# Two groups of gate columns staged in the stick-breaking and general buffers of one mixer and expert kernel

## Chip, cores and metric

The kernel runs on one core of a Trainium2 chip. The metric is the device time of one execution in microseconds (us). The kernel before took 3502.78 us, the median of three runs (3499.89 to 3507.8).

## What is computed

A decoder layer over 1024 tokens of width 1024: a norm, a token mixer with three branches (stick-breaking attention, sparse attention, a gated recurrence), a merge and an output projection, then a PEER feed-forward layer, then a final norm. The part that matters here is the last:

```python
def peer_ffn(x, w_q, sub_keys, u_tab, v_tab):
    ...
        best_s, pos = lax.top_k(cand, K)
        eidx = jnp.take_along_axis(cand_idx, pos, axis=-1)
        gate = jax.nn.softmax(best_s, axis=-1)
        ug = u_tab[eidx]
        vg = v_tab[eidx]
        hpre = jnp.einsum("nd,nhkd->nhk", xc, ug).astype(f32)
        act = (gate * jax.nn.gelu(hpre, approximate=False)).astype(x.dtype)
        return jnp.einsum("nhk,nhkd->nd", act, vg)
```

Each token has 8 heads with 16 chosen experts each, out of 16384, and each chosen expert has a gate.

## The kernel before

The 1024 tokens are cut into four parts of 256 (`PARTS`). The mixer runs part by part, as one long list of small steps (`items`), between which projections, merges and routing steps (`pieces`) are placed by estimated loads of TensorE (PE) and VectorE (DVE). The order on each engine is then settled at build time by a scheduler; on the chip each engine works through its own queue strictly in that order.

The feed-forward layer is done in two ways. For the tokens of parts 0 and 3 (256 + 256), the rows of the chosen experts are gathered one slot at a time from DRAM by GpSimd (POOL) and multiplied and summed on VectorE (`gather_tile`, lines 1149 to 1161; `gacc` is the running sum, `v_33` the row of slot 33). The gathers are spread over the whole later kernel. For the 512 tokens of parts 1 and 2 (`DENSE`), all 16384 experts are computed in 128 blocks of 128 on TensorE: `gemm1` multiplies a block of u with the tokens (`g`, line 265), ACT applies gelu (`ge`, line 1400), VectorE multiplies with the gates (`gt`, line 1434), the result is split into two half-precision parts (`ac`, lines 220 and 221), and a second product with v adds into PSUM (`acc`, line 1441). Raw weights come as `uraw` and `vraw` by SyncE's (SP's) queue and are split into two parts by ACT and VectorE (`us`, `vs`).

This needs the gates as a dense table, token by expert. `spread_pieces` (lines 1207 to 1230) makes it, four tokens a step: VectorE builds `hot` tiles of zeros and ones in one of four general buffers (tag w4, which `uraw` uses too), TensorE multiplies them into a PSUM tile `gb` (pool `ps_mm`, two buffers), ACT copies that with one instruction into a staging tile (line 1226). After four steps, 16 tokens are complete, and ACT's queue issues the write of 1 MB to the table `d_G` in DRAM (line 1228). There are 32 groups of 16 tokens. Three staging tiles serve them: two in `stages`, which share the space of the table of normalized tokens `h2` that the expert loop loads, and a third, `stage`, with one buffer. Groups 0 to 29 take turns over the three; groups 30 and 31 use the third only, since `stages` has by then to be released for `h2`. So groups 29, 30 and 31 all use `stage`:

```python
u = n0 // 16 % 3 if n0 < TH - 32 else 2
stage[0] = per.tile([128, 128, 16], F32, tag="stage", name=f"stage{n0}") if u == 2 else stages[:, u]
```

Behind the last group stands the beginning of the expert loop: three blocks of `gemm1`, then for each block k: `gemm1` of block k + 3, the load of `vraw`, at the first of every eight blocks two loads of gates (`gt_0` for the first 256 dense tokens, `gt_16` for the others, 1 MB each), the gate product, and the acc matmuls. The output projection of part 3 (`pj_wo`, `tr_wo`) is placed between blocks.

The stick-breaking branch keeps its keys in two buffers (`sbk`, 4 KB a partition each) and its values in one (`sbv`, 4 KB), and the whole mixer shares eight general buffers of 2 KB (tag `at`). After the last stick-breaking head the first three are not used again. They belong to pool `w2`, which is released together with `stage` before the expert loop's own buffers (`late`) are opened.

Of the kernel before, what the change touches and what calls it, by code (L numbers as in the profile page):

```python
# [10 lines left out]
F32 = mybir.dt.float32  # L11
# [5 lines left out]
AF = mybir.ActivationFunctionType  # L17
# [18 lines left out]
TH = 512  # L36
# [8 lines left out]
SGT, SA = 2.0 ** 10, 2.0 ** 4  # L45
# [26 lines left out]
def trunk(ctx: ExitStack, tc: tile.TileContext, a: dict, out: bass.AP):  # L72
    nc = tc.nc
    V, S, G, P = nc.vector, nc.scalar, nc.gpsimd, nc.tensor
# [13 lines left out]
    per = mix.enter_context(tc.tile_pool(name="per", bufs=1))  # L88
# [14 lines left out]
    def W4(name, shape=(128, 1024), dt=F32):  # L103
        return w4.tile(list(shape), dt, tag="w4", name=name)

    def W2(name, shape=(128, 512), dt=F32, tag="at", bufs=AT):
        return (wk if tag in ("at", "pre", "sg") else w2).tile(list(shape), dt, tag=tag, name=name, bufs=bufs)
# [98 lines left out]
    def dram(name, shape, dt=F32):  # L206
        return drm.tile(list(shape), dt, name=name)
# [92 lines left out]
    stages = hpl.tile([128, 2, 128, 16], F32, tag="h2", name="stages", bufs=1)  # L300
# [429 lines left out]
    def hg_pieces(h, pt, st):  # L730

        nm = f"hg{h}_{pt.i}"
        n = pt.n

        def pi():
            ps = proj(B_HI + h, hTs[pt.i], f"i_{nm}", pt)
            st["iT"] = PRE(f"iT_{nm}", pt)
            S.activation(st["iT"], ps, AF.Copy, scale=PS)

        def pi2():  # L740
            tr = transposed(st["iT"], f"i_{nm}", True)
            st["iv"] = W2(f"iv_{nm}", (128, n), tag="iv", bufs=2)
            S.activation(st["iv"], tr, AF.Copy)

        def pg(i, blk):
            if i == 0:
                st["raw"] = W2(f"raw_{nm}", (128, 3, n), tag="raw", bufs=2)
            ps = proj(blk + h, hTs[pt.i], f"r{i}_{nm}", pt)
            S.activation(st["raw"][:, i], ps, AF.Copy, scale=PS)

        return [pi, pi2, lambda: pg(0, B_HF), lambda: pg(1, B_HQ), lambda: pg(2, B_HG)]
# [126 lines left out]
    def gate_pieces(r, pt, st):  # L878

        def one(i):  # L880
            if i == 0:
                st["mg"] = W2(f"mg{r}_{pt.i}", (128, 6, pt.n), tag="mg", bufs=1)
            j, br = divmod(r * 6 + i, 3)
            ps = proj(B_MG + br * 8 + j, hTs[pt.i], f"mg{br}_{j}_{pt.i}", pt)
            S.activation(st["mg"][:, i], ps, AF.Copy, scale=PS)  # L885

        return [lambda i=i: one(i) for i in range(6)]
# [315 lines left out]
    d_G = dram("d_G", (32, 128, 128, 16))  # L1203
# [4 lines left out]
    def spread_pieces(pt):  # L1208

        stage = {}  # L1210

        def four(q):
            n0 = pt.t0 - TD + q * 4
            if q % 4 == 0:
                u = n0 // 16 % 3 if n0 < TH - 32 else 2
                stage[0] = per.tile([128, 128, 16], F32, tag="stage", name=f"stage{n0}") if u == 2 else stages[:, u]
            sp = spread[pt.i][:, :, q * 4:q * 4 + 4]
            hs = W4(f"hot{n0}", (128, 4, 128, 4), F16)
            V.tensor_tensor(hs[:, 0:2], iorep.unsqueeze(1).to_broadcast([128, 2, 128, 4]), sp[:, 0:2].unsqueeze(2).to_broadcast([128, 2, 128, 4]), op=ALU.is_equal)
            V.tensor_tensor(hs[:, 2:4], hs[:, 1:2].to_broadcast([128, 2, 128, 4]), sp[:, 2:4].unsqueeze(2).to_broadcast([128, 2, 128, 4]), op=ALU.mult)  # L1220
            ps = ps_mm.tile([128, 4, 128], F32, tag="mm", name=f"gb{n0}")
            for n in range(4):
                P.matmul(ps[:, n, :], hs[:, 0, :, n], hs[:, 2, :, n], start=True, stop=False)  # L1223
                P.matmul(ps[:, n, :], hs[:, 0, :, n], hs[:, 3, :, n], start=False, stop=True)
            m0 = q % 4 * 4
            S.activation(stage[0][:, :, m0:m0 + 4], ps.rearrange("p n i -> p i n"), AF.Copy, scale=SA / SGT)  # L1226
            if q % 4 == 3:
                nc.scalar.dma_start(d_G[n0 // 16], stage[0])

        return [lambda q=q: four(q) for q in range(pt.n // 4)]  # L1230

# [23 lines left out]
    def chain(fns, after=-100, before=1 << 30, deps=(), vector=False, to=None):  # L1255

        res = []
        for fn in fns:
            p = Piece(fn, after, before, list(deps) + res[-1:], vector)
            res.append(p)  # L1260
        (pieces if to is None else to).extend(res)
        return res

    def at(pt, r, kind, table, other=-10):
        i = pt.i * 4 + r
        return table.get((i // 4, i % 4, kind), other)
# [3 lines left out]
    for pt in PARTS:  # L1270
        i = pt.i
# [4 lines left out]
        for r in range(4):  # L1276
# [9 lines left out]
            p = chain(hg_pieces(r, pt, hg), ripe(at(pt, r - 2, "hg", end)), start[i, r, "hg"], here)  # L1286
            mg = None
            if r:
                mg = ({}, pt, r - 1)
                p = p + chain(gate_pieces(r - 1, pt, mg[0]), ripe(at(pt, r - 1, "hg", start)), start[i, r, "hg"], here)  # L1290
            elif i:
                prev = PARTS[i - 1]
                mg = (gates[i - 1], prev, 3)
                p = p + gates["p", i - 1]
            ng = state[i, "kv"] if r == 0 else None
            if ng is not None:
                p = p + kv[1:2]
# [49 lines left out]
    while t < N + 3 or todo:  # L1347
# [13 lines left out]
        for e, rate in (("DVE", RDVE), ("PE", RPE if t < N else REND)):  # L1361
# [5 lines left out]
            n = 0  # L1367
# [7 lines left out]
            while load_[e] < due[e]:  # L1375
                p = next((p for p in todo if not p.done and p.vector == (e == "DVE") and all(d.done for d in p.deps) and p.ready(t + 1)), None) if t < N or not n else None
# [42 lines left out]
    for k, i in enumerate(order):  # L1419
# [23 lines left out]
        for u in range(6):  # L1443
            if u in (2, 4) and len(group) == 4:
                d0 = u // 2 - 1
                ps = ps_mm.tile([128, TH], F32, tag="mm", name=f"g2_{i}_{u}")
# [124 lines left out]
```

## Time and profile before

| what | us |
|---|---|
| median of three runs | 3502.78 |
| the profiled execution | 3511.97 |
| its span | 3510.2 |
| PE busy | 3199.7 |
| DVE busy | 3000.6 |
| ACT busy | 1556.4 |
| POOL busy | 1361.7 |
| copies of groups of the third buffer (stage), 48, waiting for the write before | 11.9, 2 waits |

All times in the text below are from the profiled execution, in us from its span's start. In a timeline row stand the start, the duration, the engine, the line and the instruction, output<-input, the sizes, the count, and in brackets the idle time of the engine before it and what ended that. A name with q behind the engine (SPq, ACTq) is its queue of issued transfers. In a row of the table by stretches stand the stretch, its length, the busy time of PE, PE's weight loads, DVE, ACT and POOL with counts, the clock granted to TensorE (1.00 is full speed), the busy share of the DMA engines and GB/s. Rows of a DMA queue give packets, MB and the share of the 16 engines' time. Rows that group instructions give the busy time, the mean ns of one, and the idle time before them. The mean granted clock was 0.942.

### The profile page before, as it was taken

The page shows a single profiled execution, that of the slowest core. Times are in us where ns is not written, and L with a number is a line of the kernel's source. Part 1 is how long each engine was busy: PE and PEld are TensorE (multiplying, and loading weights), DVE is VectorE, ACT ScalarE, POOL GpSimd, SP SyncE. Part 2 cuts the span into 40 slices and gives each one's busy share as a digit, 9 for nine tenths or more (in the row PEclk, how much of TensorE's full clock was granted, in tenths as well). Part 3 has the DMA queues.
Part 4 walks back from the last instruction along what each step waited for, and adds up shares of the span by engine and source line. Part 5 has one row for each costly group of instructions (what it writes and reads, how often), then busy time and mean ns, then how long its engine had stood idle before and what let it go on. Part 6 is the DMA issues. An engine that isn't in the chain of part 4 may idle for free.

```text
span 3510.2 us, 56907 instructions
## 1 busy us (share of the span) xinstructions
PE 3199.7 (91%) x20564; PEld 2175.3 (62%) x20564; DVE 3000.6 (85%) x6666; ACT 1556.4 (44%) x3181; POOL 1361.7 (39%) x1170
## 2 busy tenths in 40 slices
PE   7999889999997799999887889889999999999998
PEld 6887777778886688888565745434444444444443
DVE  6665679888789879889997869999988998998998
ACT  5776455554543554554455233333333333333333
POOL 0000002443332322333231334357765565676672
PEclk9999999999997799999688999989999999999999
DMA  8964856889976588897574998789999999999995
GB/s 305 334 248 147 308 185 226 320 314 310 358 284 231 199 289 291 327 332 259 191 250 154 344 372 312 241 271 387 392 384 329 385 367 362 362 368 375 367 358 219
DMA packets 359283, 1058.00 MB, mean 301 GB/s; under 512 B 35236, under 2 KB 107573, under 8 KB 354391
## 3 DMA queue, kind: packets, MB, share of 16 engines
q0 software_dynamic: 147456, 536.94, 42.5%
q1 hardware_dynamic: 206934, 483.87, 38.7%
q10 hardware_dynamic: 4608, 33.56, 2.5%
q8 instruction: 161, 2.64, 0.3%
q14 instruction: 124, 1.01, 0.1%
HBM read 944.13 MB, written 110.10 MB: 300 GB/s over the span
## 4 chain that ended last, share of the span: by engine, by line
PE 49%; DVE 23%; DMA 11%; issue 8%; ACT 6%; POOL 2%; SPq 0%; DVEq 0%; POOLq 0%; ACTq 0%
PE g L265 13%; PE acc L1441 10%; PE pj_mg L265 4%; DVE u L1151 3%; DVE gacc L1161 3%; PE g L1441 3%; DMA u<-in_peer_u_dram,gidx 3%; PE pj_r_hg L265 2%; DMA v<-in_peer_v_dram,gidx 1%; PE pb L265 1%; DMA gt<-d_G 1%; PE pj_wo L265 1%; POOL v L1159 1%; PE z_sb L417 1%; DMA vraw<-in_peer_v_dram 1%
## 5 line engine op out<-in xcount | busy, mean ns | idle before, releaser
L1159 POOL DMA_INDIRECT v<-in_peer_v_dram,gidx x421 | 556.0, 1321 | 674.0 <-DVE gacc L1161 348.4
L1149 POOL DMA_INDIRECT u<-in_peer_u_dram,gidx x417 | 529.7, 1270 | 596.6 <-DVE u L1151 367.4
L265 PE MATMUL g<-h,us 128*128 128x512 f16 x3072 | 688.2, 381 | 14.8 <-ACT ge L1400 12.1
L1441 PE MATMUL acc<-vs,ac 128*128 128x512 f16 x2304 | 542.2, 383 | 39.9 <-ACT vs L220 23.5
L1441 PEld LDWEIGHTS <-ac 128*128 128x128 f16 x3072 | 303.1, 99 | 426.1 <-issue 66.8
L1161 DVE SCALAR_TENSOR_TENSOR gacc<-v,act,gacc 128x1024 f32<-128x1024 f32 x421 | 538.9, 1280 | 29.4 <-DMA v<-in_peer_v_dram,gidx 25.8
L265 PEld LDWEIGHTS <-us 128*128 128x128 f16 x3072 | 301.6, 98 | 383.0 <-issue 21.1
L1151 DVE SCALAR_TENSOR_TENSOR u<-u,gh 128x1024 f32<-128x1024 f32 x417 | 501.9, 1219 | 33.2 <-DMA u<-in_peer_u_dram,gidx 32.7
L1400 ACT ACTIVATE ge<-g 128x512 f32<-128x512 f32 x128 | 76.1, 596 | 520.7 <-PE g L265 500.1
L265 PE MATMUL pj_mg<-hT,w_mg 128*128 128x256 f16 x2304 | 273.8, 275 | 4.0 <-ACT mg L885 4.0
L265 PEld LDWEIGHTS <-w_mg 128*128 128x128 f16 x2304 | 228.2, 100 | 33.6 <-issue 6.6
L1441 PE MATMUL g<-vs,ac 128*128 128x512 f16 x768 | 190.5, 388 | 11.6 <-ACT ge L1400 11.6
L1149 POOL DMA_INDIRECT rr_u<-in_peer_u_dram,gidx x95 | 134.2, 1413 | 96.7 <-DVE rr_u L1151 49.8
L221 DVE SCALAR_TENSOR_TENSOR vs<-vraw,vs 128x1024 f16<-128x1024 f32 x128 | 154.1, 1219 | 18.6 <-ACT vs L220 18.5
L221 DVE SCALAR_TENSOR_TENSOR us<-uraw,us 128x1024 f16<-128x1024 f32 x128 | 156.1, 1219 | 10.4 <-ACT us L220 10.3
L265 PE MATMUL pb<-o,w_b 128*128 128x256 f16 x1152 | 144.7, 281 | 21.1 <-DVE sg L923 15.1
L1159 POOL DMA_INDIRECT rr_v<-in_peer_v_dram,gidx x90 | 123.0, 1367 | 102.2 <-DVE gacc L1161 81.4
L220 ACT ACTIVATE vs<-vraw 128x1024 f16<-128x1024 f32 x128 | 131.0, 1046 | 55.0 <-DMA vraw<-in_peer_v_dram 55.0
L220 ACT ACTIVATE ac<-ge 128x512 f16<-128x512 f32 x128 | 79.9, 628 | 168.3 <-DVE ge L1434 139.0
L1434 DVE TENSOR_TENSOR ge<-ge,gt 128x256 f32<-128x256 f32 x256 | 98.4, 422 | 58.7 <-ACT ge L1400 44.9
L1223 PE MATMUL gb<-hot 128*128 128x128 f16 x512 | 125.7, 294 | 24.3 <-ACT stage L1226 13.1
L220 ACT ACTIVATE us<-uraw 128x1024 f16<-128x1024 f32 x128 | 134.2, 1048 | 21.4 <-PE g L265 12.8
(1146 smaller groups left out, 6353.8 us busy)
## 6 DMA issues: line engine op xcount, KB each, us to landing
uraw<-in_peer_uT_dram SPq DMA_DIRECT2D x128, 512.0 KB, 7.7
vraw<-in_peer_v_dram SPq DMA_DIRECT2D x128, 512.0 KB, 7.2
w_mg<-dw SPq DMA_DIRECT2D x72, 512.0 KB, 5.8
gt<-d_G SPq DMA_DIRECT2D x32, 1024.0 KB, 17.5
d_G<-stages ACTq DMA_DIRECT2D x20, 1024.0 KB, 5.9
w_r_hg<-dw SPq DMA_DIRECT2D x36, 512.0 KB, 5.4
w_b<-dw SPq DMA_DIRECT2D x72, 256.0 KB, 5.5
wr_mg<-in_wblk_dram SPq DMA_DIRECT2D x24, 512.0 KB, 5.3
```

The source lines that it names most:

```text
L220: S.activation(hi, src, AF.Copy, scale=scale)
L221: V.scalar_tensor_tensor(lo, in0=src, scalar=scale, in1=hi, op0=ALU.mult, op1=ALU.subtract)
L265: P.matmul(ps, l[:, k, :], r[:, k, :], start=(i == 0), stop=(i == n - 1))
L417: P.matmul(x["z"], qz[:, hh, tl * 128:(tl + 1) * 128], st["k"][:, r0 + c0:r0 + c1], start=True, stop=(c0 > 0))
L1149: G.indirect_dma_start(out=ur, out_offset=None, in_=a["peer_u"], in_offset=bass.IndirectOffsetOnAxis(ap=idx[:, c:c + 1], axis=0))
L1151: V.scalar_tensor_tensor(ur, in0=ur, scalar=1.0, in1=h2, op0=ALU.mult, op1=ALU.mult, accum_out=hpre[:, c:c + 1])
L1159: G.indirect_dma_start(out=vr, out_offset=None, in_=a["peer_v"], in_offset=bass.IndirectOffsetOnAxis(ap=idx[:, c:c + 1], axis=0))
L1161: V.scalar_tensor_tensor(acc, in0=vr, scalar=act[:, c:c + 1], in1=acc, op0=ALU.mult, op1=ALU.add)
L1223: P.matmul(ps[:, n, :], hs[:, 0, :, n], hs[:, 2, :, n], start=True, stop=False)
L1400: S.activation(ge, ps, AF.Gelu, scale=1.0 / (SW * SH2))
L1434: V.tensor_tensor(gv, gv, gt[:, :, i % 8, :], op=ALU.mult)
L1441: P.matmul(ps, ac[:, x, t * 128:(t + 1) * 128], v[:, y, dh * 512:(dh + 1) * 512], start=start and n == 0, stop=stop and n == 2)
```

## The change

Group 30 is staged in the two key buffers, half of the 128 expert rows each. Group 31 is staged in the value buffer (half) and in two of the eight general buffers (a quarter each). ACT's copy of each step becomes two or three instructions, one for each piece, and the write becomes two or three transfers, of 512 KB or 256 KB. Groups 0 to 29 stay as they were. What is computed is the same.

```diff
             if q % 4 == 0:
-                u = n0 // 16 % 3 if n0 < TH - 32 else 2
-                stage[0] = per.tile([128, 128, 16], F32, tag="stage", name=f"stage{n0}") if u == 2 else stages[:, u]
+                u = n0 // 16 % 3
+                if n0 < TH - 32:
+                    stage[0] = [per.tile([128, 128, 16], F32, tag="stage", name=f"stage{n0}") if u == 2 else stages[:, u]]
+                elif n0 < TH - 16:
+                    stage[0] = [W2(f"stage{n0}_{i}", (128, 64, 16), tag="sbk", bufs=2) for i in range(2)]
+                else:
+                    stage[0] = [W2(f"stage{n0}", (128, 64, 16), tag="sbv", bufs=1)] + [W2(f"stage{n0}_{i}", (128, 32, 16)) for i in range(2)]
...
             m0 = q % 4 * 4
-            S.activation(stage[0][:, :, m0:m0 + 4], ps.rearrange("p n i -> p i n"), AF.Copy, scale=SA / SGT)
-            if q % 4 == 3:
-                nc.scalar.dma_start(d_G[n0 // 16], stage[0])
+            i0 = 0
+            for s in stage[0]:
+                i1 = i0 + s.shape[1]
+                S.activation(s[:, :, m0:m0 + 4], ps[:, :, i0:i1].rearrange("p n i -> p i n"), AF.Copy, scale=SA / SGT)
+                if q % 4 == 3:
+                    nc.scalar.dma_start(d_G[n0 // 16][:, i0:i1], s)
+                i0 = i1
```

The scheduler settles the order anew, and it differs from the last groups on. Lines from 1222 on have numbers higher by 5 to 9 in the new kernel. Three places follow.

TensorE, behind the product of block 3 (g_3), before: the transpose tr_wo, the 24 matmuls of pj_wo, the next tr_wo and the 24 of g_4 stand ahead of the first acc.

```order
L265 MATMUL g_3_23023<-h_22904,us_23026 128x512
L282 MATMUL tr_wo_3_23086<-packed,y_3_22760 128x128 x2
L265 LDWEIGHTS w_wo_3_23091
L265 MATMUL pj_wo_3_23093<-m_21853,w_wo_3_23091 128x256
...
L282 MATMUL tr_wo_3_23120<-packed,y_3_22848 128x128 x2
L265 LDWEIGHTS us_23129
L265 MATMUL g_4_23126<-h_22904,us_23129 128x512
...
L1441 MATMUL acc_23014<-vs_23056,ac_23065 128x512
```

The same place now, where line 1450 is the acc product:

```order
L265 MATMUL g_3_23041<-h_22922,us_23044 128x512
L282 MATMUL tr_wo_3_23104<-packed,y_3_22760 128x128 x2
L1450 LDWEIGHTS ac_23083
L1450 MATMUL acc_23032<-vs_23074,ac_23083 128x512
...
L265 LDWEIGHTS w_wo_3_23109
L265 MATMUL pj_wo_3_23111<-m_21853,w_wo_3_23109 128x256
```

The 18 matmuls of the first block's acc have moved ahead of pj_wo, and 18 more (the second block) ahead of g_4.

VectorE, at the last hot tiles (lines 1219 and 1220), before:

```order
L1161 SCALAR_TENSOR_TENSOR gacc_33806<-v_24_33880,act_33418,gacc_33806 128x1024
L1220 TENSOR_TENSOR hot_22864<-hot_22864,spread_20612 128x1024
L1161 SCALAR_TENSOR_TENSOR gacc_33806<-v_25_33883,act_33418,gacc_33806 128x1024
L1161 SCALAR_TENSOR_TENSOR gacc_33806<-v_26_33886,act_33418,gacc_33806 128x1024
L1219 TENSOR_TENSOR hot_22877<-iorep,spread_20612 128x1024
L1219 TENSOR_TENSOR hot_22890<-iorep,spread_20612 128x1024
L1220 TENSOR_TENSOR hot_22877<-hot_22877,spread_20612 128x1024
L1220 TENSOR_TENSOR hot_22890<-hot_22890,spread_20612 128x1024
```

The same place now, where lines 1224 and 1225 are the hot tiles:

```order
L1161 SCALAR_TENSOR_TENSOR gacc_33824<-v_24_33898,act_33436,gacc_33824 128x1024
L1225 TENSOR_TENSOR hot_22874<-hot_22874,spread_20612 128x1024
L1224 TENSOR_TENSOR hot_22904<-iorep,spread_20612 128x1024
L1225 TENSOR_TENSOR hot_22889<-hot_22889,spread_20612 128x1024
L1161 SCALAR_TENSOR_TENSOR gacc_33824<-v_25_33901,act_33436,gacc_33824 128x1024
L1225 TENSOR_TENSOR hot_22904<-hot_22904,spread_20612 128x1024
L1161 SCALAR_TENSOR_TENSOR gacc_33824<-v_26_33904,act_33436,gacc_33824 128x1024
```

The last hot tiles have moved ahead of the gathered row v_26. Further on, the last accumulation ahead of the first gate product was that of v_37 and is now that of v_33. In the loop the difference is made up by the fifth block, then grows to eight more (block 72) and turns into five fewer (block 124).

SyncE's queue, at the first gates, before:

```order
L100 DMA uraw_23250<-in_peer_uT_dram 128x1024
L255 DMA w_wo_3_23091<-dw_68_5687 128x2048
L100 DMA uraw_23339<-in_peer_uT_dram 128x1024
L100 DMA uraw_23463<-in_peer_uT_dram 128x1024
L100 DMA vraw_23054<-in_peer_v_dram 128x1024
L1429 DMA gt_0_23059<-d_G 128x16x128
L1429 DMA gt_16_23061<-d_G 128x16x128
```

The same place now, where line 1438 is the load of the gates:

```order
L100 DMA uraw_23268<-in_peer_uT_dram 128x1024
L100 DMA uraw_23357<-in_peer_uT_dram 128x1024
L100 DMA vraw_23072<-in_peer_v_dram 128x1024
L1438 DMA gt_0_23077<-d_G 128x16x128
L1438 DMA gt_16_23079<-d_G 128x16x128
L100 DMA vraw_23175<-in_peer_v_dram 128x1024
L255 DMA w_wo_3_23109<-dw_68_5687 128x2048
```

One uraw and the weights w_wo_3 (dw_68) of the next pj_wo have moved behind the gates.

## The prediction

> **What bounds the kernel now.** I read the page first (busy times and the chain that ended last), then the chain piece by piece, then the engines' timelines around the two groups that the change touches, and last the transfers there.
>
> ```profile
> span 3510.2 us, 56907 instructions
> PE 3199.7 (91%) x20564; PEld 2175.3 (62%) x20564; DVE 3000.6 (85%) x6666; ACT 1556.4 (44%) x3181; POOL 1361.7 (39%) x1170
> PE 49%; DVE 23%; DMA 11%; issue 8%; ACT 6%; POOL 2%; SPq 0%; DVEq 0%; POOLq 0%; ACTq 0%
> ```
>
> TensorE (PE) is the bound over the whole, VectorE (DVE) close behind it. The change sits at one seam, 2009 to 2075 us, where the mixer ends and the expert loop begins. The timeline of ScalarE (ACT) there shows what the staging buffer costs:
>
> ```profile
> 2013.06 0.33 ACTq L1228 DMA_DIRECT2D d_G<-stage  x1
> 2024.21 1.09 ACT L1226 ACTIVATE stage<-gb 128x512 f32<-128x512 f32 x2 [8.76 <-DMA d_G<-stage]
> 2034.00 1.09 ACT L1226 ACTIVATE stage<-gb 128x512 f32<-128x512 f32 x2 [3.13 <-DMA d_G<-stage]
> ```
>
> Group 29's write leaves at 2013.06; the first copy of group 30 wants the same buffer and waits 8.76 us for it to land. Group 31 waits 3.13 us for group 30's. TensorE has two PSUM buffers for these products and stops behind ACT:
>
> ```profile
> 2024.86 0.28 PE L1223 MATMUL gb<-hot 128*128 128x128 f16 x1 [7.94 <-ACT stage L1226]
> 2026.74 3.72 PE L265 MATMUL pj_wo<-m,w_wo 128*128 128x256 f16 x24
> 2034.65 0.28 PE L1223 MATMUL gb<-hot 128*128 128x128 f16 x1 [2.30 <-ACT stage L1226]
> 2036.41 0.29 PE L1224 MATMUL gb<-hot 128*128 128x128 f16 x1
> 2062.40 0.38 PE L282 MATMUL tr_wo<-packed,y 128*128 128x128 f32 x2
> 2063.25 2.78 PE L265 MATMUL pj_wo<-m,w_wo 128*128 128x256 f16 x24 [0.47 <-ACT ge L1400]
> 2066.50 5.34 PE L265 MATMUL g<-h,us 128*128 128x512 f16 x24 [0.25 <-ACT y L935]
> 2074.18 7.94 PE L1441 MATMUL acc<-vs,ac 128*128 128x512 f16 x36 [2.34 <-ACT ac L220]
> ```
>
> So 7.94 + 2.30 = 10.2 us of TensorE idle belong to the buffer. But the seam has a second gate, the last row: the first expert product (acc) needs the gate table gt of all 512 tokens. It comes through SyncE's (SP's) queue behind the loads of expert weights (uraw), whose buffers VectorE's splits (us) free, and VectorE waits for its second half:
>
> ```profile
> 2048.91 2.43 DVE L221 SCALAR_TENSOR_TENSOR us<-uraw,us 128x1024 f16<-128x1024 f32 x2
> 2050.16 1.54 SPq L100 DMA_DIRECT2D uraw<-in_peer_uT_dram  x2
> 2052.22 11.87 SPq L1429 DMA_DIRECT2D gt<-d_G  x2
> 2072.97 1.43 DVE L1434 TENSOR_TENSOR ge<-ge,gt 128x256 f32<-128x256 f32 x4 [0.82 <-DMA gt<-d_G]
> ```
>
> gt leaves at 2052.22, lands at 2072.97, and acc follows 2074.18 - 2072.97 = 1.2 us later. Between them TensorE had other work to do (rows of 2063.25 and 2066.50), so only 2.34 us of idle show. And the transfers are full:
>
> ```profile
> 2024.00:2037.00 13.00, 9.55 (x72) 8.33 (x71) 8.75 (x9) 4.62 (x9) 6.13 (x6) 0.76 0.96 365
> 2037.00:2052.00 15.00, 12.46 (x48) 4.99 (x49) 9.06 (x8) 6.34 (x8) 4.47 (x3) 0.82 1.02 393
> 2052.00:2075.00 23.00, 19.90 (x104) 10.13 (x104) 13.23 (x22) 6.39 (x10) 6.26 (x4) 1.00 1.09 360
> ```
>
> The last two columns are the DMA engines' busy share (0.96, 1.02, 1.09) and GB/s. From 2024 on the seam is bound by transfers as much as by the buffer.
>
> **The change, part by part.** *The wait that goes.* The key and value buffers were last read here:
>
> ```profile
> L417 PE MATMUL z_sb<-k_sb,qz x192: 275/592/1222, 118.1 to 1921.1; 128*128 128x512 f32 x96, 128*128 128x128 f32 x32, 128*128 128x256 f32 x32, 128*128 128x384 f32 x32
> L447 PE MATMUL ov_sb<-v_sb,aT_sb x576: 219/275/476, 135.1 to 1935.8; 128*128 128x64 f32 x192
> ```
>
> Both ended 80 us before group 30 begins, so the copies go ahead and the last gb starts 10.2 us earlier, at 2026.2. What is late next there is VectorE's last hot tile; before, it stood behind a gathered row that came late:
>
> ```profile
> 2025.49 1.29 DVE L1161 SCALAR_TENSOR_TENSOR gacc<-v,act,gacc 128x1024 f32<-128x1024 f32 x1 [2.46 <-DMA v<-in_peer_v_dram,gidx]
> 2026.70 1.29 DVE L1219 TENSOR_TENSOR hot<-iorep,spread 128x1024 f16<-128x1024 f16 x2
> ```
>
> In the new order all hot tiles stand ahead of that row (v_26), so they are done by about 2025.5 and 10.2 us can be had.
>
> *The copies in pieces.*
>
> ```profile
> L935 ACT ACTIVATE y<-pj_wo 128x256 f32<-128x256 f32 x32 | 12.2, 381 | 35.9 <-PE pj_wo L265 35.9
> L1226 ACT ACTIVATE stage<-gb 128x512 f32<-128x512 f32 x48 | 28.4, 598 | 52.5 <-PE gb L1224 40.6 <-DMA d_G<-stage 11.9
> ```
>
> Group 30: 4 x (2 x 381 - 598) = 0.7 us more. Group 31: a piece of 256 and two of 128 columns; on the line through these two rows a 128 costs 381 - 109 = 272 ns, so 4 x (381 + 544 - 598) = 1.3 us; if a 128 cost as much as a 256, 4 x 545 = 2.2 us. Three more issues of 0.33 us on ACT's queue make 1 us. What is queued behind them is the split of the first expert weights (us), which waits for its own load; ACT is busy 4.62 of 13 us there. I take 0; at most 0.7 + 2.2 = 2.9 us, if every copy stood in TensorE's way.
>
> *The writes in pieces.* The bytes are the same. The queues in 2024 to 2075:
>
> ```profile
> q1 hardware_dynamic: 7302, 8.90, 51.3%
> q0 software_dynamic: 2181, 7.89, 40.8%
> ...
> uraw<-in_peer_uT_dram SPq DMA_DIRECT2D x9, 512.0 KB, 11.0
> ```
>
> q1 (SP) moved 8.90 MB in 51.3% of 51 us, 2.94 us per MB; q0 (gathers) 20.8 us for 7.89 MB, 2.64 us per MB. The half-megabyte loads in q1 show no penalty against the whole, so I take 0 for pieces of 512 and 256 KB, with 1 us either way. [...] No run here shows pieces of this write.
>
> *When gt lands.* The new SP order asks for one uraw less and puts w_wo_3 (dw_68) behind gt. Every load before it moves with the gb steps, which free the buffers. If all of it moves by 10.2 us, and by another 1.2 us (half of the 2.43 of 2048.91) since gt no longer waits for one more split, gt's second half lands at 2072.97 - 11.4 = 2061.6. The other end is transfer time: ahead of gt then stand four gathers fewer (the new VectorE order has v_33 rather than v_37 last before the gates) and two loads of 0.52 MB fewer: 4 x 0.52 x 2.64 + 2 x 0.52 x 2.94 = 5.5 + 3.1 = 8.6 us, so 2064.4. I take 2062.5, nearer the first, since the share of 0.96 ahead of 2037 leaves a little room; ends kept for the range: 2058 (loads quicker than before) and 2073 (nothing gained).
>
> *What stands behind the wait for gt.* This is the part that eats the gain. Before, pj_wo and the product g_4 stand ahead of acc on TensorE, 2063.25 to 2066.50 + 5.34 = 2071.84, or 8.6 us of work. In the new order acc stands ahead of both, and they are queued behind its wait. acc at 2062.5 + 1.2 = 2063.7 with 8.6 us still to do equals 2072.3 of before, against 2074.18: a gain of 1.9 us out of 10.2.
>
> *The clock.* g_3 ended at 2062.4 and would end 10.2 us earlier, at 2052.2, so TensorE then idles some 11 us. What that costs is in the stall that is removed:
>
> ```profile
> 2024.80:2027.00 2.20, 2.14 (x18) 2.08 (x18) 1.50 (x2) 1.14 (x4) 0.00 (x0) 0.50 1.00 410
> ```
>
> After 7.94 us of idle the granted clock was 0.50, and the pj_wo of 2026.74 took 3.72 instead of 2.78 us: 2.2 x 0.5 + 0.94 = 2.0 us lost. Before, that loss was covered by the wait for gt; now it falls behind it, on the path: +2.0 us, at least 0, at most 2.5.
>
> *The gathers put off.*
>
> ```profile
> 2057.95 1.28 DVE L1161 SCALAR_TENSOR_TENSOR gacc<-v,act,gacc 128x1024 f32<-128x1024 f32 x1 [0.75 <-DMA v<-in_peer_v_dram,gidx]
> 2075.00:2200.00 125.00, 121.58 (x678) 68.16 (x677) 110.06 (x243) 48.27 (x70) 52.52 (x39) 1.00 0.91 321
> ```
>
> Four accumulations of 1.28 us, 5.1 us of VectorE, move into the first expert blocks. There VectorE is busy 110.06 of 125 us, 14.9 us free: I take 0, at most 5.1 if they come ahead of what TensorE needs. At the end the new order has five gathers more behind block 124 than before, 6.4 us; cover is VectorE's idle there:
>
> ```profile
> 3479.34 0.16 DVE L237 TENSOR_TENSOR gu_fin<-gy_fin 128x1 f32<-128x1 f32 x1 [2.27 <-ACT gy_fin L235]
> 3488.85 1.34 DVE L1470 SCALAR_TENSOR_TENSOR yd<-acc,yd 128x512 f32<-128x512 f32 x2 [4.69 <-PE acc L1441]
> ```
>
> 2.27 + 4.69 = 7.0 us, just enough: 0, at most 3. Between them the expert loop keeps its work but many splits and accumulations change places; TensorE's largest wait there was
>
> ```profile
> PE acc L1441 <- ACT vs L220: 23.5, 8, 6.2
> ```
>
> 23.5 us in 8 waits, up to 6.2 each. One more or one less of these is 6 us either way, and the order doesn't say which.
>
> *The sum.* -1.9 (gt) + 2.0 (clock) + 0 + 0 = +0.1 us. The profiled execution took 3512.0 us around its span of 3510.2; the median of the runs is 3502.8. I put the change on the median: 3502.9, say **3503 us, no change**.
>
> **The rivals.** *Faster: the 10.2 us pass through.* gt would have to land by 2052.2, 10.3 us before my value. For it: a load in the seam took 11.0 us (the median of nine, above), much of it in line behind others, and four gathers are gone. Against: shares of 1.02 and 1.09. Time: 3502.8 - 10.2 = 3492.6. A lucky order in the expert loop (one 6.2 us wait less, and 2 us at the seam) comes to 3495.
>
> *Slower: TensorE stands in front of acc.* The place is acc behind g_3. The sum is even when gt lands at 2062.4; every us after that is lost, because nothing else is ahead of acc. If the room of the four gathers goes to others and gt lands at 2070, the loss is 7.6 us: 3510.4. At the old 2073 it is 10.6 us: 3513.4. For it: in-order TensorE and full transfers. Against: the writes really leave earlier. The put-off gathers on the path (5.1 + 3) would give 3511.
>
> *The change does nothing:* if the new buffers were still held, ACT would wait as before, 3502.8. The rows of 1921 and 1936 speak against it; the general buffers, used by two quarter pieces, have no such row. It falls within the forecast.
>
> **How the numbers follow.** A measurement of this kernel can tell about 0.2% (7 us) from no change. Forecast (a wash at the seam, within 7 us, the idle buffers' case included): 0.50. Faster: gain passes through 0.17, lucky order 0.13; 0.30. Slower: TensorE in front of acc 0.11, gathers or an unlucky order 0.09; 0.20. The forecast's own range is 3496 to 3510. For 8 in 10 it must reach most of both sides: 3490 (the full 10.2 and a little from the order) to 3513 (gt at its old time).
>
> **What would show it.** Right: no d_G<-stage wait left on ACT for groups 30 and 31; the last gb near 2026; acc with an idle time of about 11 us in front of it and a clock near 0.5 just behind; acc near 2064; the first pj_wo behind it near 2068. Wrong: acc before 2058 (then faster by as much), or after 2068 (slower); a TensorE without idle before acc; waits of TensorE in the expert loop that differ by more than 5 us from before, in which case the order there, not the seam, decided.

## The result, and the profile after

| kernel | median, us | lowest to highest | runs | ratio to before, 95% interval |
|---|---|---|---|---|
| before, beside it | 3503.36 | 3499.89 to 3507.8 | 6 | |
| changed | 3528.77 | 3515.17 to 3532.32 | 6 | 1.0062, 1.0045 to 1.0080 |
| changed, once more, later | 3526.59 | 3519.36 to 3535.12 | 7 | 1.0058, 1.0037 to 1.0080 |

The change makes the kernel 0.6% slower, about 22 us (0.0062 x 3503; the two medians are 25.4 us apart), where no change was forecast. The page of the changed kernel, as the lines of before:

```profile
span 3525.8 us, 56950 instructions
PE 3206.4 (91%) x20564; PEld 2177.9 (62%) x20564; DVE 2998.0 (85%) x6666; ACT 1550.6 (44%) x3190; POOL 1333.6 (38%) x1170
```

TensorE is busy for 6.7 us more with the same instructions, which fits a slower clock behind more waits: the mean granted clock is 0.940, against 0.942 before. At the seam, the timelines of ACT, PE, SP and DVE of the changed kernel read:

```profile
2012.49 0.84 ACTq L1236 DMA_DIRECT2D d_G<-stage  x2
2016.72 0.72 ACT L1234 ACTIVATE stage<-gb 128x256 f32<-128x256 f32 x3 [0.56 <-PE gb L1229]
2025.66 1.06 ACT L220 ACTIVATE us<-uraw 128x1024 f16<-128x1024 f32 x1 [5.35 <-DMA uraw<-in_peer_uT_dram]
```

```profile
2026.77 1.04 PE L265 MATMUL g<-h,us 128*128 128x512 f16 x2 [7.22 <-ACT us L220]
2028.03 22.00 PE L265 MATMUL g<-h,us 128*128 128x512 f16 x94 [0.22 <-DVE us L221]
2056.36 6.78 PE L1450 MATMUL acc<-vs,ac 128*128 128x512 f16 x18 [6.11 <-ACT ac L220]
2062.98 2.78 PE L265 MATMUL pj_wo<-m,w_wo 128*128 128x256 f16 x24
2065.81 4.05 PE L1450 MATMUL acc<-vs,ac 128*128 128x512 f16 x18
```

```profile
2035.59 7.27 SPq L1438 DMA_DIRECT2D gt<-d_G  x2
2055.15 1.43 DVE L1443 TENSOR_TENSOR ge<-ge,gt 128x256 f32<-128x256 f32 x4 [4.03 <-DMA gt<-d_G]
```

No copy waits for a write any more. In their place TensorE waits 7.22 us for the first expert weights (uraw, through us) and 6.11 us for gt (through ac), and the first acc takes 6.78 us where the next takes 4.05.

To see where time goes, I compare when TensorE has done equal work, counted in matmul columns. Single executions drift apart ahead of the seam, where the program is the same: this profile is 8.0 us ahead of that of before at 2000 us. So I set the difference to 0 there. Times in the first column are those of before; a plus is a loss against it.

| before, us | changed | changed again | e1 | e2 | e4 | k31 | k57 | f1 | f2 |
|---|---|---|---|---|---|---|---|---|---|
| 2100 | +0.5 | -1.0 | -0.7 | +5.4 | +0.3 | -0.1 | -1.4 | +1.5 | +5.8 |
| 2200 | +8.6 | +7.1 | -0.7 | +13.9 | +1.0 | +9.0 | +5.4 | +7.7 | +9.0 |
| 2350 | +10.3 | +10.7 | +2.3 | +14.7 | -0.1 | +9.9 | +11.0 | +13.6 | +11.1 |
| 2550 | +12.8 | +18.0 | +2.3 | +18.3 | -0.1 | +10.3 | +14.4 | +14.0 | +11.1 |
| 2700 | +22.6 | +25.7 | +2.3 | +23.7 | -0.1 | +10.3 | +22.4 | +21.8 | +11.1 |
| 3000 | +32.8 | +37.0 | +3.0 | +27.3 | -3.6 | +9.1 | +21.3 | +12.6 | +29.6 |
| 3488 | +22.9 | +29.1 | +0.9 | +19.3 | -6.1 | +6.3 | +20.4 | +18.7 | +31.8 |

Behind the seam, at 2100, the changed kernel is where it was: +0.5. The loss comes in the expert loop behind it, whose work is unchanged. What TensorE waits for from 2075 us on, in the views of waits (us in total, times, longest), first before, then changed:

```profile
PE acc L1441 <- ACT vs L220: 23.5, 8, 6.2
PE g L1441 <- ACT ge L1400: 11.6, 3, 6.5
PE g L265 <- ACT ge L1400: 11.1, 2, 5.9
PE acc L1441 <- DVE vs L221: 8.7, 7, 2.9
```

```profile
PE acc L1450 <- ACT vs L220: 21.2, 7, 6.5
PE g L1450 <- ACT ge L1409: 14.6, 4, 7.5
PE acc L1450 <- DVE vs L221: 11.5, 6, 3.0
PE g L265 <- ACT ge L1409: 10.9, 2, 5.5
PE g L265 <- ACT p L1459: 7.5, 2, 6.3
PE acc L1450 <- ACT ac L220: 4.2, 2, 3.1
PE g L265 <- DVE ts L986: 3.4, 2, 2.0
```

No single row grew by more than 7.5 us; all rows together grew from 63.4 to 78.6 us. With the slower matmuls behind them that is about what the table shows: between 2100 and 3488 the same work takes 22.4 us longer (22.9 - 0.5), in which TensorE is busy 6.6 us longer and idle 15.8 us longer. The loop has little room for such waits. Three stretches before the change (PE, PEld, DVE, ACT, POOL busy, clock, DMA share, GB/s), and the same after it:

```profile
2150.00:2250.00 100.00, 91.23 (x469) 48.10 (x468) 99.12 (x348) 25.89 (x37) 36.24 (x28) 0.97 0.74 249
2350.00:2450.00 100.00, 100.00 (x466) 45.32 (x464) 95.92 (x161) 35.79 (x50) 70.29 (x49) 1.00 1.00 372
2550.00:2650.00 100.00, 100.00 (x465) 45.31 (x464) 87.77 (x140) 33.65 (x46) 59.42 (x41) 1.00 0.97 364
```

```profile
2150.00:2250.00 100.00, 90.25 (x451) 46.82 (x450) 98.63 (x338) 25.62 (x36) 34.51 (x29) 0.95 0.73 241
2350.00:2450.00 100.00, 100.00 (x465) 45.35 (x464) 90.83 (x157) 36.47 (x50) 62.52 (x43) 1.00 0.96 345
2550.00:2650.00 100.00, 92.34 (x420) 41.28 (x419) 80.22 (x131) 28.90 (x40) 56.18 (x40) 0.97 0.97 355
```

DVE is full in the first stretch, TensorE and the transfers in the others.

### The profile page after: what moved, and what is told of

It is laid out like the page before. It is cut to its first block, busy times and chain, and to the rows that moved or that the text cites. A ratio compares the mean times of both kernels' runs of the same rounds, so it can differ in the third digit from the quotient of the medians.

```text
span 3525.8 us, 56950 instructions
## 1 busy us (share of the span) xinstructions
PE 3206.4 (91%) x20564; PEld 2177.9 (62%) x20564; DVE 2998.0 (85%) x6666; ACT 1550.6 (44%) x3190; POOL 1333.6 (38%) x1170
## 5 line engine op out<-in xcount | busy, mean ns | idle before, releaser
L1159 POOL DMA_INDIRECT v<-in_peer_v_dram,gidx x421 | 532.5, 1265 | 699.3 <-DVE gacc L1161 395.1
L265 PE MATMUL g<-h,us 128*128 128x512 f16 x3072 | 696.5, 384 | 29.2 <-ACT ge L1409 10.9
L265 PEld LDWEIGHTS <-w_mg 128*128 128x128 f16 x2304 | 227.5, 100 | 31.8 <-issue 5.4
L265 PE MATMUL pj_r_hg<-hT,w_r_hg 128*128 128x256 f16 x1152 | 142.6, 282 | 3.8 <-ACT raw_hg L749 3.5
```

The costliest lines, as they stand in the source:

```text
L265: P.matmul(ps, l[:, k, :], r[:, k, :], start=(i == 0), stop=(i == n - 1))
L1159: G.indirect_dma_start(out=vr, out_offset=None, in_=a["peer_v"], in_offset=bass.IndirectOffsetOnAxis(ap=idx[:, c:c + 1], axis=0))
```

## The experiments

**Staging and order apart (e1, e2).** The build settles the order of each engine's instructions anew, so the change is two things: other buffers, and another order of all that follows. To part them, the order is fixed by hand: from the seam on, each instruction is tied behind the one that stands ahead of it in the wanted order, for issue alone and without a wait for its result.

```diff
+            ins = lists[e][at]
+            if prev is not None:
+                tc.add_manual_dep(ins, prev.name, mybir.DependencyInfo(mybir.DependencyClass.NoSync, mybir.DependencyReason.DATA), reason="order")
+            prev = ins
```

The list of places (at) is that of before for e1, which keeps the new staging, and that of the changed kernel for e2, which keeps the old staging.

> The changed kernel with its staging (groups 30 and 31 in the freed buffers), but from the seam on every engine's instructions stand in the order that they had before the change (the added pieces of a copy or of a write stand where the whole one stood). Theory A (the 25 us come from the new order of the expert loop, which the build settles, and not from the staging): 3490 to 3505 us, that is as fast as before, or up to 10 us faster, since pj_wo and g_4 stand ahead of acc again while gt lands about 10 us earlier; no loss against before between 2100 us and the end. Theory B (the staging itself costs the time: earlier and smaller writes, other buffers, transfers that collide in the loop): 3520 to 3535 us, as the changed kernel. In between, 3508 to 3517 us: both take part.

> The kernel before with its one staging buffer for the last groups, but from the seam on every engine's instructions stand in the order of the changed kernel. Theory A (order): 3523 to 3540 us: the 20 to 25 us that the changed kernel loses in the expert loop, and at the seam up to 10 us more, because acc now waits for gt without pj_wo and g_4 ahead of it and the wait for the staging buffer is back. Theory B (staging): 3500 to 3507 us, as before; with the seam's part alone 3503 to 3515 us, and in the loop no loss beyond 5 us after 2100 us.

| ratio to before | before's order | changed order |
|---|---|---|
| one staging buffer | 1 | 1.0102 (1.0087 to 1.0117), 3539.59 us |
| freed buffers | 0.9993 (0.9984 to 1.0002), 3503.43 us | 1.0062 (1.0045 to 1.0080), 3528.77 us |

Theory A holds: the order alone costs 0.7% with the new staging and 1.0% with the old (that the instructions are tied costs nothing in e1). The staging itself saves 0.4% under the changed order, and under before's order at most 0.2%. Why not 10 us there? The rows of e1 at the seam (ACT, DVE, DVE, PE):

```profile
2024.87 1.06 ACT L220 ACTIVATE us<-uraw 128x1024 f16<-128x1024 f32 x1 [0.46 <-DMA uraw<-in_peer_uT_dram]
2031.35 1.28 DVE L1161 SCALAR_TENSOR_TENSOR gacc<-v,act,gacc 128x1024 f32<-128x1024 f32 x1 [1.57 <-DMA v<-in_peer_v_dram,gidx]
2032.55 2.35 DVE L221 SCALAR_TENSOR_TENSOR us<-uraw,us 128x1024 f16<-128x1024 f32 x2
2033.82 22.58 PE L265 MATMUL g<-h,us 128*128 128x512 f16 x94 [6.81 <-DVE us L221]
```

uraw is there at 2024.87, but DVE splits it only at 2032.55: accumulations that wait for gathered rows stand ahead. TensorE waits 6.81 us. That is a wait in the place of the one removed.

**The seam with either order, the loop with before's (e3, e4, e7).** All three have the new staging. e4 has the changed order up to block 4's ge*gt, e3 only up to the first ge*gt, so that pj_wo and g_4 stand ahead of acc again; behind, both have before's order. e7 is e3 with SP's loads in before's order throughout:

```diff
 SP
+w_wo5
 uraw6
+uraw7
 vraw0
 gt0, first half
 gt0, second half
 vraw1
-w_wo5
-uraw7
```

> The changed kernel with its staging; up to the first multiplication ge*gt every engine keeps the order of the changed kernel (its gathers on DVE stand behind the us splits), from there on every engine has the order from before (pj_wo and g_4 ahead of acc, and the expert loop as before). Theory A (the loss sits in the loop's order): the two gaps of the seam go both. The run with before's order throughout lost 6.8 us in front of g, because four gathers on DVE stood ahead of the us split; without them 3503.4 - 6.8 = 3497 us, 3493 to 3500. Rival (the gathers that are put off are missed later, since DVE has no room in the loop): 3501 to 3510 us, with new waits for us or ac between 2050 and 2400 us.

> The changed kernel with its staging and its own order up to the fifth block's ge*gt (so acc stands ahead of pj_wo and g_4 as in the changed kernel), and before's order of the rest of the expert loop. Theory A (the seam is a wash as forecast, the loss comes from the loop's order behind it): 3500 to 3507 us, no loss beyond 5 us against before from 2100 us to the end. Rival (the seam shifts the loop against its transfers, whatever the order there): 3515 us or more, with losses near 2150 and 2560 us as in the changed kernel.

> As the run with the seam of the changed kernel and before's order behind it, with one thing more: SP's loads stand in before's order throughout, so that the load of w_wo5 stands ahead of uraw6 again (in that run pj_wo waited 10.4 us for it). On DVE the gathers stay behind the us splits. Theory A: the 10.4 us in front of pj_wo go, the 6.8 us in front of g stay away, the loop is before's: 3494 to 3501 us, that is 0.1 to 0.3 per cent faster than before. Rival (the expert loop is held by its transfers, so that time won at the seam is lost at the next transfer that is late): 3502 to 3508 us, with losses against before between 2075 and 2350 us.

| | median, us | ratio to before |
|---|---|---|
| e3 | 3509.03 | 1.0008 (0.9994 to 1.0021) |
| e4 | 3508.60 | 1.0006 (0.9995 to 1.0018) |
| e7 | 3504.57 | 0.9997 (0.9982 to 1.0012) |

e4 has the changed kernel's seam and is as fast as before: the loss lies behind the fifth block. But the gain expected of e3 and e7 isn't there. In e3 pj_wo met a load that was late, as SP's order had it behind gt:

```profile
2061.22 4.02 PE L265 MATMUL pj_wo<-m,w_wo 128*128 128x256 f16 x18 [10.40 <-DMA w_wo<-dw]
```

In e7 that wait is gone, and these two stand there:

```profile
2033.38 1.03 PE L265 MATMUL g<-h,us 128*128 128x512 f16 x2 [6.56 <-ACT us L220]
2070.34 4.91 PE L1450 MATMUL acc<-vs,ac 128*128 128x512 f16 x15 [3.31 <-ACT ac L220]
```

6.56 us for the first uraw, 3.31 us for gt with pj_wo and g_4 already done: in each of these three the last wait of the seam is for a transfer. My expectation was wrong in taking the transfers to be early.

**Single places of the loop (e5, e6, e8, e11, e12).** In the changed order two to five more gather steps on DVE stand ahead of most us splits of blocks 10 to 77. e5 puts them back behind in blocks 9 to 24 and 31 to 53; e6 puts them ahead in the kernel before. e8 moves two pairs of loads in SP's queue, e11 and e12 the splits of vs on ACT and DVE, with one matmul of acc.

```diff
 DVE, e5, block 43
-gather step, gather step, gather step, ge39, ge39, us43
+ge39, ge39, us43, gather step, gather step, gather step
 SP, e8
+gt8, second half
 vraw10
 w_pq2
 vraw11
-gt8, second half
+vraw40
+vraw41
 uraw47
-vraw40
-vraw41
 ACT, e11, behind us46
-vs40, vs41, p7_39_2, ac41, ac42, p7_39_4
+p7_39_2, vs40, ac41, ac42, vs41, p7_39_4
```

> The changed kernel with its own order on all engines, except that on DVE, in blocks 9 to 24 and 31 to 53, the one to five gather steps that stand ahead of a us split beyond the number there before the change are put right behind it. Theory D (those steps, 1.2 us each, make the us splits late, their raw buffers come free late, the next uraw load waits in SP's queue, and the vraw loads behind it come late): 3511 to 3520 us, the loss of 9.7 us near 2560 us gone and perhaps part of that near 2150. Rival (another engine's order, or SP's own, carries the loss): 3525 to 3532 us.

> The mirror image: the kernel before, with its staging and its order, except that on DVE in blocks 31 to 53 three to five gather steps more stand ahead of each us split, as many as in the changed kernel. Theory D: 3511 to 3518 us, with a new wait of acc for vs near 2555 us, about 8 to 10 us with the slower clock behind it, and an uraw load that holds SP's queue for over 15 us ahead of it. Rival (the place of the gathers does nothing by itself): 3500 to 3506 us.

> The changed kernel with its own order on all engines but for two places in SP's queue: the load of gt for blocks 8 to 15 (its second half) stands ahead of vraw10 instead of behind vraw11, and vraw40 and vraw41 stand ahead of uraw47, which waited 18.7 us for a free buffer with these two behind it. Theory Q (the order of SP's queue carries these two losses): the 3.1 us wait of acc near 2142 us and the 6.5 us wait of acc near 2569 us go, with the slower clock behind them: 3528.8 - 7 - 9.7 = 3512 us, 3508 to 3519. Rival (DVE is late there whatever comes in): the waits move to the next blocks, 3522 to 3532 us.

> The changed kernel once more, for comparison on the same chip with the runs beside it: 3522 to 3533 us, and its two waits of acc near 2142 us and 2569 us again, if they belong to its order and not to one execution.

> The changed kernel, except at one place of the loop, the stretch between the us splits of blocks 46 and 47: there ACT and DVE have before's order (p7_39_2, the copy that frees g's PSUM buffer, stands ahead of the splits vs40 and vs41 again, instead of behind them), and on TensorE the one matmul of acc for block 40 that stands ahead of g of block 43 goes behind it. Theory V (a vs split whose load comes late holds ACT's queue, with the copy behind it that TensorE needs to go on with g; with the copy ahead, g of block 43 covers the wait): the loss of 7.7 to 9.7 us between 2550 and 2575 us goes, all else stays: 3526.6 - 8 = 3518.5 us, 3515 to 3522. Rival (the late load is the price, and its wait only moves behind g): 3523 to 3530 us, with a wait of acc for vs at the same block.

> As the run before, and the same in seven more stretches (between the us splits 32-33, 43-44, 48-49, 50-51, 58-59, 86-87 and 90-91): ACT and DVE take the order that vs, ac and p7 had there before the change; SP, POOL, the gathers on DVE and the rest of TensorE keep the changed kernel's. Theory V: beyond block 40 also part of the 8 to 9 us between 2975 and 3010 us (g waits 6.9 us for p there) and little elsewhere: 3508 to 3517 us. Rival: within 3 us of the run before.

| | median, us | ratio to before |
|---|---|---|
| e5 | 3536.36 | 1.0093 (1.0071 to 1.0115) |
| e6 | 3514.61 | 1.0031 (1.0018 to 1.0045) |
| e8 | 3524.67 | 1.0058 (1.0038 to 1.0079) |
| changed again | 3526.59 | 1.0058 (1.0037 to 1.0080) |
| e11 | 3526.64 | 1.0062 (1.0048 to 1.0076) |
| e12 | 3525.10 | 1.0055 (1.0040 to 1.0069) |

These came from the place near 2569 us in the changed kernel (SP, SP, SP, ACT, PE, PE):

```profile
2523.02 0.33 SPq L100 DMA_DIRECT2D uraw<-in_peer_uT_dram  x1
2532.74 4.72 SPq L1438 DMA_DIRECT2D gt<-d_G  x2
2537.51 18.72 SPq L100 DMA_DIRECT2D uraw<-in_peer_uT_dram  x1
2567.78 1.06 ACT L220 ACTIVATE vs<-vraw 128x1024 f16<-128x1024 f32 x1 [12.46 <-DMA vraw<-in_peer_v_dram]
2568.89 0.59 PE L1450 MATMUL acc<-vs,ac 128*128 128x512 f16 x1 [6.48 <-ACT vs L220]
2570.65 4.55 PE L265 MATMUL g<-h,us 128*128 128x512 f16 x13 [1.17 <-ACT p L1459]
```

A load of uraw (that of block 47) stands 18.72 us in SP's queue, two loads of vraw behind it come late, ACT stands 12.46 us at vs, and behind vs stands p, the copy that frees the buffer for g. So TensorE can go on neither with acc nor with g.

The expectations of e5, e8 and e10 take such a stand for a wait for a free buffer. The trace shows it otherwise. The buffer of this load was free from 2534.18 on, the end of DVE's split of block 43 (2532.97 + 1.21). The load ahead of it, that of block 46 (the first row), did start when its buffer came free: it left at 2523.02, behind the split of block 42, which ended at 2521.78 + 1.21 = 2522.99, and took 0.33 us. What stands ahead of the held load are the two loads of gates. In e8, where the load of vraw for block 40 has taken that place, it is this one that is held, from 1.4 us after its buffer came free (at 2545.37):

```profile
2541.65 4.99 SPq L1438 DMA_DIRECT2D gt<-d_G  x2
2546.73 12.82 SPq L100 DMA_DIRECT2D vraw<-in_peer_v_dram  x1
```

From 2100 us on, all 27 issues of SP's queue that take over 4 us before the change, and 28 of 29 after it, are the second gate load of a pair or the issue directly behind the pair. So e8 only changed which load is held there. e10 (below) makes the same move at eight places, all behind such a pair. No run moved the vraw loads ahead of the gates; what that would win isn't known, and why the queue is held there isn't shown.

Theory D (gathers) and Q (SP's queue, as tested) fail as explanations of the time. In the measure of the table of equal work, e5 has no loss left between 2550 and 2700 (+33.7 at both) but loses 15 us between 2200 and 2350. e8 loses 3.5 us up to 2200 instead of 7 to 9, since acc, which in the changed kernel waits 3.10 us for gt at 2142, has no idle time in front of it there (2143.39), but 10.4 up to 2350, as the changed kernel does, and near 2569 it has the same waits as the changed kernel's second profile (2.07 us for vs where that has 2.06, 2.67 for p in both). Yet the mirror e6 did cost 0.3%, within the range that Theory D gave it, so the place of the gathers isn't free. Its profile waits at a place of its own, not near 2555:

```profile
2471.80 4.29 PE L1441 MATMUL g<-vs,ac 128*128 128x512 f16 x12 [6.04 <-ACT ge L1400]
```

That profile has lost 7.2 us by 2550 and only 0.1 by 3488, so it doesn't show where the 0.3% of the timed runs goes.

For Theory V the two profiles disagree. The changed kernel again, then e11, in one stretch:

```profile
2545.00:2580.00 35.00, 30.27 (x129) 12.96 (x127) 27.28 (x45) 8.43 (x13) 19.90 (x15) 0.90 1.03 387
```

```profile
2545.00:2580.00 35.00, 35.00 (x164) 15.85 (x163) 29.84 (x50) 11.24 (x16) 22.98 (x16) 1.00 1.03 395
```

TensorE is busy throughout in e11 and does 35 matmuls more; in the measure of the table the 7.7 to 9.8 us lost here are gone (+13.3 at 2550 and at 2700). But e12, which has the same mend here, loses 5.2 us between 2550 and 2700, with the wait of acc for vs behind g that the rival named:

```profile
2567.64 0.38 PE L1450 MATMUL acc<-vs,ac 128*128 128x512 f16 x1 [1.72 <-ACT vs L220]
```

The timed runs don't show the mend: 1.0062 against 1.0058 and 1.0062 unmended, and the times of both runs fall into the rival's range. Whether the time is lost again later in most executions, one profile can't say. e12, with seven more places mended, isn't told from e11 either.

**Where along the loop (k31, k57).** The changed order up to block 31 or 57, before's order behind.

> The changed kernel with its own order up to the multiplication ge*gt of block 31, and before's order of everything behind it. With the cut at block 4 it was 3508.6 us. Theory S (the loss is the sum of waits along the whole loop): the waits near 2142, 2163, 2290 and 2302 us are in, those behind are not: 3512 to 3520 us. Theory L (only the late half, where g runs less far ahead of acc, costs): 3503 to 3511 us.

> As the run before with the cut at block 57, so that the waits near 2477 and 2569 us are in as well. Theory S: 3517 to 3526 us, more than the run before by 4 to 10 us. Theory L: 3503 to 3513 us.

k31: 3516.06 us, 1.0045 (1.0030 to 1.0059). k57: 3525.95 us, 1.0059 (1.0045 to 1.0074). With e4 as the cut at block 4, the ratios rise 1.0006, 1.0045, 1.0059, and 1.0062 for the whole. Theory L fails, and Theory S holds, but not evenly. Some 14 us fall to blocks 5 to 31 (2088 to 2455 us), and this step is clear of the intervals; in the profiles some 10 us of it are lost by 2350, where DVE is full. From k31 to k57 it is 5 us by the ratios and 10 by the medians, but the two intervals overlap, and nothing is to be told behind. (The changed kernel's two profiles lose some 10 us more up to 3000 and win 8 to 10 back by 3488.)

**Is it this order, or any new one (f1, f2)?** Each half of the change alone, with the order that the build then settles.

```diff
 f1
                 else:
-                    stage[0] = [W2(f"stage{n0}", (128, 64, 16), tag="sbv", bufs=1)] + [W2(f"stage{n0}_{i}", (128, 32, 16)) for i in range(2)]
+                    stage[0] = [per.tile([128, 128, 16], F32, tag="stage", name=f"stage{n0}")]
 f2
                 elif n0 < TH - 16:
-                    stage[0] = [W2(f"stage{n0}_{i}", (128, 64, 16), tag="sbk", bufs=2) for i in range(2)]
+                    stage[0] = [per.tile([128, 128, 16], F32, tag="stage", name=f"stage{n0}")]
```

> One half of the change alone: group 30 goes to the two key buffers in two pieces, group 31 to the staging buffer, which group 29 has left by then, so that neither group waits for it. The order is the build's own. Theory N (any newly settled order loses what before's order had, and TensorE shows it by how far g runs ahead of acc: 501 blocks in sum, as 498 in the changed kernel): 3516 to 3532 us, like the changed kernel, with the two waits at the seam gone as there. Rival (the loss belongs to the changed kernel's own order, or to group 31's three pieces): 3498 to 3508 us.

> The other half alone: group 30 stays in the staging buffer and waits for group 29's write as before (8 us at the seam), group 31 goes to the value buffer and two general ones in three pieces. The order is the build's own, g ahead of acc by 489 blocks in sum, less than in any other. Theory N: 3518 to 3540 us. Rival: 3500 to 3510 us.

f1: 3526.08 us, 1.0067 (1.0054 to 1.0080), with no wait for the buffer left at the seam. f2: 3535.27 us, 1.0082 (1.0067 to 1.0097), with 9.32 us of wait left there. So three newly settled orders lose 0.6 to 0.8%, each with waits of its own. Theory N holds for these three, which are orders of one edit and its halves; whether before's order is an unusually good one isn't shown. Its measure, how far g runs ahead of acc, fails. Counted in the traces at the first matmul of each block's acc, in blocks and in sum, g is 536 ahead before and 512, 509 and 499 in f1, the changed kernel and f2 (the expectations' own count is some 10 lower). But it is 532 in k31 and 528 in k57, which lose 0.45% and 0.59%: most of the loss with most of the lead. Which property of the order costs the time stays open; that its place is mostly blocks 5 to 31 is shown.

**A version that is no slower (e10).** e7, with two loads of vraw moved ahead of a uraw that is held in SP's queue, at eight places of the loop.

```diff
 SP
+vraw40
+vraw41
 uraw47
-vraw40
-vraw41
```

> As the run with the seam mended, and at eight places of the loop (ahead of uraw39, 47, 63, 79, 87, 103, 111 and 119, each of which waits 5 to 16 us for a free buffer in SP's queue) the two vraw loads that stood behind stand in front. Theory Q: the waits of acc for vs behind these places (3.8 us near 2981, 3.7 near 3140, 3.8 near 3230, 6.4 near 3322 in the run with before's order) shrink, 5 to 15 us less than the run with the seam mended alone: 3482 to 3494 us. Rival (the transfers are full, so what one load gains another loses): within 3 us of the run with the seam mended, or slower, since uraw comes later.

3500.44 us, 0.9984 (0.9971 to 0.9998). It is the fastest here, by 0.16% over before, at the edge of what is measured, and not told from e7 on the same chip (3504.57). The 5 to 15 us expected of the loads are not there; the loads of vraw now stand directly behind the gate loads, where e8 held one for 12.82 us.

## Why the prediction was wrong

**The step that failed** is the last of the part on the gathers: "One more or one less of these is 6 us either way, and the order doesn't say which." The term was put at nothing, and "gathers or an unlucky order" together got 0.09. e1 and e2 set it at 25 us with the new staging (3528.8 against 3503.4) and 34 with the old (3539.6 against 3505.5). The error lay in taking many exchanged places as one wait with either sign. All three orders that the build settled anew cost 22 to 29 us, in a loop where TensorE, DVE and the transfers are each full in turn; by what property of the order stays open. The prediction had one stretch that hinted at it (2075 to 2200 us, DVE busy 110.06 of 125 us), but this mean hides that DVE is full from 2150 on (99.12 of 100 us), and it looked at no stretch of the loop behind it.

**The wait that goes: right.** No write is waited for, and the last copy of gb ends at 2020.31 (2020.03 + 0.28); with the 8.0 us by which this execution was ahead that is 2028.3, against 2036.74 + 0.60 = 2037.3 before, 9.0 us earlier where 10.2 was forecast.

**What is late next: half right.** I named the hot tiles. They were on time. The first uraw was not: 7.22 us in front of g, a term that the sum lacked. It cost nothing there, since acc waits for gt in any case, and it is the reason why the idle time in front of acc was 6.11 us instead of some 11.

**When gt lands: right.** Forecast 2062.5; 2055.15 + 8.0 = 2063.2. acc, forecast near 2064: 2056.36 + 8.0 = 2064.4.

**What stands behind gt: right.** acc stood alone at the gate, and pj_wo followed at 2062.98 + 8.0 = 2071.0, not 2068, by the clock's term and the later gate.

**The clock: mis-sized.** The row, with 6.3 us of near idleness ahead:

```profile
2050.00:2056.30 6.30, 0.25 (x3) 0.01 (x1) 1.98 (x7) 1.22 (x3) 0.00 (x0) 0.90 1.05 380
2056.30:2063.20 6.90, 6.84 (x21) 2.66 (x22) 3.85 (x6) 2.51 (x5) 0.00 (x0) 0.59 1.10 339
```

6.78 - 4.05 = 2.7 us instead of 2.0, with a granted clock of 0.59.

**Copies and writes in pieces: right, nothing to see.** Three pieces took 0.72 us, where 0.93 was reckoned (381 + 544 ns), against 0.60 for a whole copy, all hidden. The transfers, with the median from issue to landing at the end:

```profile
d_G<-stage ACTq DMA_DIRECT2D x10, 1024.0 KB, 6.9
d_G<-stage ACTq DMA_DIRECT2D x3, 512.0 KB, 8.2
d_G<-stage ACTq DMA_DIRECT2D x2, 256.0 KB, 12.7
```

The pieces landed later than the median whole write, but in the crowd of the seam, where the three whole writes before the change took 6.3 to 11.1 us, and gt was on time.

**The seam's sum: right.** Forecast +0.1 us; the two profiles show +0.5 and -1.0 at 2100.

**The rivals.** "The 10.2 us pass through" needed gt by 2052: e7 shows that even with pj_wo and g_4 ahead, acc waits for gt. "TensorE stands in front of acc" happened, and was paid by the copies that no longer wait, as the forecast had it. The forecast named a difference of TensorE's waits in the loop by over 5 us as the sign that the order, not the seam, decided: they grew by 78.6 - 63.4 = 15.2 us.

## What to carry to other kernels

Where a build settles the order, an edit is two changes; tie the old order to the new code and the new order to the old code before you credit or blame the edit. Give a newly settled order a price of its own, and a range with room for it when TensorE, VectorE and the transfers are full behind the edit: here the price was 22 to 29 us, where TensorE's longest single wait was 6.5 us before. A single wait mended in such a loop was gone in one profile and not in the time, so judge a mend by timed runs alone. And before a long row of a queue is called a wait for a buffer, look up when that buffer came free.

## What was not expected of the hardware

Profiles of kernels whose program is the same up to the seam stood between 12.1 us ahead and 2.9 us behind that of before at 2000 us, so times of two profiles are compared only from a common point on. On SP's queue the issue directly behind a pair of gate loads took up to 18.72 us in the changed kernel and up to 15.55 before. The uraw load of 18.72 us had its buffer free. Moving two loads of vraw ahead (e8) got a vraw load held for 12.82 us, its buffer free too, and bought no time (1.0058, as the changed kernel's 1.0058 and 1.0062).
